# An expert layer's branches rearranged: the first up and its hint ahead of the arms, both products turned ahead of the third up, and the residual at an earlier place

## The chip, the cores and the metric

The kernel runs on one core of one Trainium2 chip. The metric is the device time of one execution in microseconds, the median of several runs. The kernel is a program of one core; its five engines are TensorE (PE in the profile), VectorE (DVE), ScalarE (ACT), GpSimd (POOL) and SyncE (SP), and each runs its own list of instructions in order. They wait for each other through semaphores.

## The reference

One decoder layer on 256 tokens of 1024 channels in float32: a token mixer, a cross-attention and a mixture of experts, each followed by a layer norm over the scaled residual. The change touches only the last part:

```python
def moe_ffn(x, router_w, router_b, w_gu, b_gu, w_dn, b_dn):
    logits = x2 @ router_w + router_b
    top_v, top_i = lax.top_k(logits, 4)          # 4 of 32 experts
    gate = jax.nn.softmax(top_v, axis=-1)
...
    def expert_block(args):
        gu = xb @ w_gu[e] + b_gu[e]              # 1024 -> 2048
        g, u = gu[:, :1024], gu[:, 1024:]
        g = jnp.minimum(g, 7.0); u = jnp.clip(u, -7.0, 7.0)
        h = (u + 1.0) * g * jax.nn.sigmoid(1.702 * g)
        return (h @ w_dn[e] + b_dn[e]) * gb[:, None]
...
x = layer_norm(alpha * x + moe_ffn(x), norm_g[2], norm_b[2])
```

Each expert has 8 MB of weights for the first product (gate and up, "gu") and 4 MB for the second ("down"), so the 32 experts read 384 MB. How many tokens an expert gets is known only when the router has run.

## The kernel before

The mixer and the attention take the first 370 us or so and are not touched. Behind them `Moe.run` goes through the 32 experts, in an order that begins at expert 16; "place e" below is the e-th expert in that order, from 0 to 31.

**Weights.** `load(e)` issues the 12 transfers of an expert, 1 MB each, on SP's queue: eight gu slots (line 1017), then four slots with a pair of down blocks each (line 1024). They go into a ring of 19 buffers of 1 MB, all called `w`. SP issues strictly in order, and a transfer into a buffer waits until the instructions that read the buffer's former content are over. With 12 slots for each place, slot n waits for the readers of slot n - 19: the eighth gu slot of place e + 1 waits for those of the first gu slot of place e. `ring_of(True)` takes a buffer out of the ring for good.

**The work of a place.** An expert's tokens are gathered in blocks. The first 32 are the "first up" (`upper(bank, 0, ..)`: 32 fp32 matmuls of line 1220 over the eight gu slots, which the trace records as 64, with a bias product of line 1224), then `act` (clipping, sigmoid and product on DVE and ACT, lines 1191 to 1199; its result is `uc`, the product), `hT_of` (transposes of line 91, which turn the product) and `rows_down` (16 matmuls of line 1265 over the down slots, 32 in the trace), with the sum into `ye` by ACT and DVE (line 1240). Every second place `combine` (line 1276) adds the outcome of the last two places into the output in four PSUM banks, and the other places gather the rows of the next two experts (`take`, line 1076, and `turn`, line 91, with the scaling of lines 1092 and 1094).

**The arms.** Since the count n of a place is data, each place has branches on PE, ACT and DVE: `If(n > 32)`, labelled `more`, with inside it `If(n > 64)`, labelled `most`. This gives three arms. None (n up to 32): first up, product, downs. Some (33 to 64): first up, second up of the next 32 tokens, two products, two downs. Many (over 64): as some, with a third block of 32 tokens that is gathered, turned, sent through the gu slots once more (the "third up", matmuls g<-w,xTo), and through the downs by `block_down`. In the trace a third up stands at three places only, 12, 16 and 25. In this kernel the first up stands inside each of the arms; a branch prefetch hint for the next place's branch, `soon(following)`, stands in each arm but the many arm, and one for `most` at the head of the `more` arm.

**The residual.** At place 20 (`MID`) `residual()` runs ahead of the loads: DVE spreads the norm's rows on diagonals (line 987), PE broadcasts them (line 990), ACT copies them to `gb`, and POOL makes the scaled residual `x2` (lines 994, 997). `gb` and `x2` are two buffers taken out of the ring for good, so it has 17 from there on. At places 22 and 24 `add` sums `x2` into the output banks (line 1009), at 22 POOL's queue brings the last norm's rows, and at 26 `last_rows` (line 1004) broadcasts them into `gb`. `finish` normalises the output after the last place; ahead of it stands a branch `rest` for counts over 96.

## Time and profile before

| | us |
|---|---|
| median of 3 runs | 1511.12 |
| lowest and highest run | 1500.52 to 1512.25 |
| the profiled execution's own time | 1505.24 |
| its span | 1503.3 |
| PE busy | 1240.6 (83%) |
| DVE busy | 612.3 (41%) |
| ACT busy | 360.4 (24%) |
| POOL busy | 137.6 (9%) |

The transfers moved 470.20 MB, on average 313 GB/s over the span. The span runs from the first instruction to the last one on the core. A row of a timeline gives the start, the duration, the engine, the line and operation, what is written and read (out<-in by the program's names, partitions x elements), the number of instructions in the row, and in brackets the idle time ahead of it with what ended it. "issue" there is time in which the engine waited for nothing that the profile shows. On SP's queue a row of transfers lasts from the first to the last issue of its group, the waits between them included.

### The profile page before, as it was taken

Reading aid. Unit: us, or ns where it says so; the run is one execution under the profiler, and the core shown is the slowest. Engines: PE = TensorE matmul, PEld = TensorE weight load, DVE = VectorE, ACT = ScalarE, POOL = GpSimd, SP = SyncE. Lnnn points to the kernel's source line nnn. Section 1 sums busy time; section 2 is a strip of 40 time slices with the busy share of each in tenths; the row PEclk is TensorE's granted clock in tenths of the full one; section 3 lists DMA queues with packets and bytes.
Section 4 is the critical chain, followed back from the end, with each engine's and each line's share of the span. In section 5 each row is a group of like instructions: output and inputs, shape, how many; then the busy total and the mean of one; then the engine's idle time right before and its main releaser. Section 6 shows DMA issues by size and latency. Waiting matters only on the chain. (4 is left out here: it accounts for less than half of the span.)

```text
span 1503.3 us, 21051 instructions
## 1 busy us (share of the span) xinstructions
PE 1240.6 (83%) x8396; PEld 614.9 (41%) x8396; DVE 612.3 (41%) x1346; ACT 360.4 (24%) x725; POOL 137.6 (9%) x139
## 2 busy tenths in 40 slices
PE   8878999999988877787779487859788888788774
PEld 8768979999852212221222132213222222222111
DVE  4999875685453222222222232214322323123124
ACT  4424564545331111111111011102211112112101
POOL 3993000000030000000000000000020000000001
PEclk9989999999978988989999799979899999699898
DMA  9526627656859999999996899779969998569991
GB/s 304 155 71 147 206 83 194 213 172 219 306 217 414 415 416 416 413 416 417 415 416 280 321 408 415 300 299 416 417 252 415 415 414 342 221 264 415 416 415 63
DMA packets 110187, 470.20 MB, mean 313 GB/s; under 512 B 12081, under 2 KB 16276, under 8 KB 77244
## 3 DMA queue, kind: packets, MB, share of 16 engines
q1 hardware_dynamic: 108028, 462.53, 78.7%
q0 software_dynamic: 1712, 4.26, 1.3%
q8 instruction: 114, 1.87, 0.5%
q10 hardware_dynamic: 272, 1.05, 0.2%
q14 instruction: 61, 0.50, 0.1%
HBM read 466.49 MB, written 1.31 MB: 311 GB/s over the span
## 5 line engine op out<-in xcount | busy, mean ns | idle before, releaser
L1220 PE MATMUL g<-w,xT 128*32 128x512 f32 x2048 | 291.3, 681 | 125.0 <-DMA w<-in_expert_w_gu_dram 62.6
L1265 PE MATMUL m<-w,hT 128*32 128x512 f32 x1472 | 213.4, 674 | 9.5 <-DVE ye L1240 6.2
L1220 PEld LDWEIGHTS g<-w,xT 128*32 128x32 f32 x2048 | 63.4, 118 | 326.8 <-issue 209.5
L1191 DVE TENSOR_SCALAR gc<-g 64x256 f32<-64x256 f32 x70 | 29.2, 416 | 378.4 <-PE g L1220 278.9
L142 DVE TENSOR_TENSOR wl<-w,wh 128x1024 fp32r<-128x1024 f32 (+1 forms) x96 | 114.4, 1228 | 67.8 <-ACT wh L80 67.8
L1192 ACT ACTIVATE row<-gc 64x256 f32<-64x256 f32 x92 | 38.4, 418 | 386.5 <-DVE gc L1191 386.5
L80 ACT ACTIVATE wh<-w 128x1024 fp32r<-128x1024 f32 (+1 forms) x112 | 105.8, 992 | 102.1 <-PE big L172 66.4
L1240 DVE TENSOR_TENSOR ye<-ye,m 32x512 f32<-32x512 f32 x86 | 58.5, 680 | 167.1 <-ACT ye L80 165.9
L172 PE MATMUL big<-xh,wh 128*128 128x256 f32 x352 | 102.3, 291 | 0.0
L172 PE MATMUL big<-xl,wh 128*128 128x256 f32 x352 | 101.8, 289 | 0.0
L172 PE MATMUL big<-xh,wl 128*128 128x256 f32 x352 | 101.8, 290 | 0.0
L1265 PEld LDWEIGHTS m<-w,hT 128*32 128x32 f32 x1472 | 48.4, 121 | 115.5 <-issue 97.4
L80 ACT ACTIVATE ye<-m 32x512 f32<-32x512 f32 x86 | 50.7, 590 | 176.1 <-PE m L1265 175.1
L1220 PE MATMUL u<-w,xT 128*32 128x512 f32 x704 | 82.1, 607 | 0.0
L91 PE MATMUL m<-ident,uc 64*128 64x64 f32 x172 | 29.0, 250 | 50.5 <-ACT hT L80 31.3
L172 PEld LDWEIGHTS big<-xl,wh 128*128 128x128 f32 x352 | 69.4, 197 | 1.1 <-issue 0.8
L172 PEld LDWEIGHTS big<-xh,wh 128*128 128x128 f32 x352 | 69.5, 198 | 0.3
L172 PEld LDWEIGHTS big<-xh,wl 128*128 128x128 f32 x352 | 69.0, 197 | 1.3 <-issue 1.2
L1276 PE MATMUL y<-ye,pgT 128*128 128x512 f32 x128 | 60.3, 613 | 3.1 <-DVE ye L1240 2.1
L994 POOL TENSOR_TENSOR w<-w,row 128x512 f32<-128x512 f32 x4 | 5.2, 1328 | 589.1 <-DMA w<-in_expert_w_gu_dram 589.1
L1092 DVE TENSOR_SCALAR xT<-m,rowc 128x128 f32<-128x128 f32 x64 | 22.1, 406 | 84.0 <-PE m L91 72.8
L91 PEld LDWEIGHTS m<-ident,uc 64*128 64x128 f32 x172 | 17.3, 140 | 86.1 <-ACT hT L80 44.2
(429 smaller groups left out, 1799.7 us busy)
## 6 DMA issues: line engine op xcount, KB each, us to landing
w<-in_expert_w_gu_dram SPq DMA_DIRECT2D x256, 1024.0 KB
w<-in_expert_w_down_dram SPq DMA_DIRECT2D x127, 1024.0 KB
w<-in_w_in_dram SPq DMA_DIRECT2D x23, 1024.0 KB
w<-in_xa_wkv_dram SPq DMA_DIRECT2D x8, 1024.0 KB
w<-in_w_branch_dram SPq DMA_DIRECT2D x4, 1024.0 KB
w<-in_w_out_dram SPq DMA_DIRECT2D x4, 1024.0 KB
w<-in_xa_wq_dram SPq DMA_DIRECT2D x4, 1024.0 KB
w<-in_xa_wo_dram SPq DMA_DIRECT2D x4, 1024.0 KB
```

Source lines behind the costliest of these rows:

```text
L80: self.nc.scalar.activation(out, in_, AF.Copy, scale=scale)
L91: self.nc.tensor.transpose(out, in_, self.ident[0:k, 0:k])
L142: eng.tensor_tensor(out=l[:, js, :n], in0=t[:, js, :n], in1=h[:, js, :n].bitcast(F32), op=ALU.subtract)
L172: self.last = nc.tensor.matmul(dst, l, r, start=(b not in seen), stop=(last and i == 2), skip_group_check=True)
L994: self.nc.gpsimd.tensor_tensor(out=x2[:, t, s], in0=self.x2h[:, t, s].bitcast(F32), in1=self.x2l[:, t, s].bitcast(F32), op=ALU.add)
L1092: self.nc.vector.tensor_scalar(out, in_, g, t, op0=ALU.mult, op1=ALU.add)
L1191: nc.vector.tensor_scalar_min(gc[0:n, s], g[:, s], 7.0)
L1192: nc.scalar.activation(sg[0:n, s], gc[0:n, s], AF.Sigmoid, scale=1.702)
L1220: nc.tensor.matmul(gu[32 * c:32 * c + 32, :], xT[:, k, :], W[k][:, c * 512:c * 512 + 512], start=(k == 0), stop=(k == 7), skip_group_check ...
L1240: nc.vector.tensor_add(ye[:, c, :], ye[:, c, :], pd[64 * c:64 * c + 32, :])
L1265: self.nc.tensor.matmul(pd[p0:p0 + w, :], hT[:, j, h * w:h * w + w], W[8 + k][:, c * 512:c * 512 + 512], start=(i < P // (2 * w)), stop=(i ...
L1276: self.nc.tensor.matmul(self.y[t][c][:], pgT[rows, t, :], ye[rows, v, :], start=False, stop=last, skip_group_check=True)
```

## The change

The diff does six things:

- `residual()` moves from ahead of the loads of place 20 to behind those of place 6, into two ring buffers that go back to the ring; both `add` follow at place 7, where before they were at 22 and 24.
- The two buffers that stay out of the ring, `gb` and `o`, are taken at place 31, behind its loads; the norm's rows come into a tile `ends` (the buffer of `xno`), and `last_rows` runs there, where before it was at 26.
- The first up of each place from 1 on stands ahead of the branch `more`, once, and no longer in both arms. Its hint, `soon(f"more{e}")`, stands just ahead of it. The hints at the ends of the arms, and the one for `rest`, are gone. Place 0 gets a hint `early`.
- In the many arm both products are turned (`hT_of`) into the halves of one tile `both` before the third up, and the gates of its rows (`gates_of`) are turned there too.
- In the many arm `act` of the third block stands ahead of the two downs, not between them.
- `rows_down` takes the turned product and no longer turns it itself.

```diff
...
 FIRST = 16
-MID = 20
+MID = 6
...
                 if when == k:
                     fn()
-    def rows_down(self, W, uc, r, between=()):
+    def rows_down(self, W, hT, r, between=()):
         nc = self.nc
-        hT = self.hT_of(uc, 32)
         pd = self.pm.tile([P, 512], F32, name="m")
         self.down(W, [(hT, 32, pd)], between)
         ye = self.ye[r:r + 32]
...
         for c in range(2):
             nc.vector.tensor_add(ye[:, c, :], ye[:, c, :], pd[64 * c:64 * c + 32, :])
-    def hT_of(self, uc, w):
+    def hT_of(self, uc, w, hT=None):
         nc, f = self.nc, self.f
         n = 2 * w
         b = self.pm.tile([P, 512], F32, name="m")
-        hT = self.wk.tile([P, 4, P], F32, name="hT")
+        if hT is None:
+            hT = self.tile("hT", [P, 4, P])
         for i in range(2):
             for j in (2 * i, 2 * i + 1):
                 f.transpose(b[:, j * n:j * n + n], uc[0:n, j * P:j * P + P])
...
         gu = self.up(e, W, blocks, self.places(blocks))[0]
         return self.act(gu, w, self.tile("uc", [P, 512], bufs=2))
-    def block_down(self, e, W, pe, uc, w, name="xno"):
-        pgT = self.gates_of(e, pe, w)
+    def block_down(self, e, W, pe, uc, w, name="xno", pgT=None):
+        if pgT is None:
+            pgT = self.gates_of(e, pe, w)
         pd = self.pm.tile([P, 512], F32, name="m")
         self.down(W, [(self.hT_of(uc, w), w, pd)])
         ye = self.tile(name, [P, D])
...
         nc.vector.tensor_copy(self.cnt[:, 0:E], self.cf[:])
         nc.vector.tensor_reduce(self.cnt[:, E:E + 1], self.cf[:], axis=AX.X, op=ALU.max)
         xT2 = xT, xT1
+        tc.mark_branch_hint_location("early", "LikelyTaken", engines=[ENG.PE])
         self.gather_T(pe, *xT2, 0)
         for t in range(2):
             for c in range(2):
...
             tc.mark_branch_hint_location(label, "LikelyTaken", engines=[ENG.PE])
+        def rows_of(keep=False):
+
+            return self.ring_of(keep)[:].rearrange("p a b -> p (a b)").rearrange("p (t d) -> p t d", t=2)
+
         count(0)
         for e in range(E):
-            if e == MID:
-                gb, x2 = (self.ring_of(True)[:].rearrange("p a b -> p (a b)").rearrange("p (t d) -> p t d", t=2) for _ in range(2))
-                self.residual(gb, x2)
             x = order[e]
             W = self.load(x, e == E - 1)
+            if e == MID:
+                gb, x2 = rows_of(), rows_of()
+                self.residual(gb, x2)
             first, end, lead = e == 0, e == E - 1, e % 2 == 0
             c = 0 if lead else CAP
             ahead = not lead and not end
...
                 for j, at in ((1, 0), (2, 2), (3, 4)):
                     hooks.append((at, lambda j=j: self.gather_T(pe0, *xT2, j)))
                 hooks.append((5, gates_all))
-            if e in (MID + 2, MID + 4):
-                self.add(x2, (e - MID) // 2 - 1)
-                if e == MID + 2:
-                    for i, name in enumerate(('norm_g', 'norm_b')):
-                        nc.gpsimd.dma_start(x2[i:i + 1, 0, :], self.I[name][2:3, :])
-            if e == MID + 6:
-                self.last_rows(gb, x2[0:2, 0, :])
+            if e == MID + 1:
+                for t in range(2):
+                    self.add(x2, t)
+            if end:
+                ends = self.tile("xno", [P, D])
+                for i, name in enumerate(('norm_g', 'norm_b')):
+                    nc.gpsimd.dma_start(ends[i:i + 1, :], self.I[name][2:3, :])
+                gb, o = rows_of(True), rows_of(True)
+                self.last_rows(gb, ends[0:2, :])
             if not end:
                 count(e + 1)
             bank, other = self.gu()
-            following = "rest" if end else f"more{e + 1}"
             product = lambda gu: self.act(gu, 32, self.tile("uc", [P, 512], bufs=2))
             def middle():
...
             if first:
-                with tc.If(n > 32):
+                with tc.If(n > 32, label="early"):
                     self.early(x, W, 32)
                     with tc.If(n > CAP):
                         self.early(x, W, CAP)
                 upper(bank, 0, hooks)
                 for t in range(2):
                     bias(t)
-                soon(following)
                 self.ye = self.tile("ye", [P, 2, 512])
                 nc.vector.memset(self.ye[:], 0.0)
                 uc = product(bank)
                 middle()
-                self.rows_down(W, uc, c, turns())
+                self.rows_down(W, self.hT_of(uc, 32), c, turns())
             else:
+                soon(f"more{e}")
+                upper(bank, 0, hooks)
                 with tc.If(n > 32, label=f"more{e}") as some:
                     soon(f"most{e}")
-                    upper(bank, 0, hooks)
                     peo = self.onehot(self.halves("peo", 32), [(x, CAP, 32, 0)])
                     uc = product(bank)
                     upper(other, 1)
                     uc2 = product(other)
                     with tc.If(n > CAP, label=f"most{e}") as many:
-                        xo, xTo = self.tile("xno", [P, D]), self.tile("xTo", [P, 8, 32])
+                        xo = self.tile("xno", [P, D])
                         for h in range(2):
                             self.take(peo, xo, h)
                         middle()
+                        both = self.tile("hT", [P, 4, P])
+                        hT = self.hT_of(uc, 32, both[:, :, 0:64])
+                        pgTo = self.gates_of(x, peo, 32)
+                        xTo = self.tile("xTo", [P, 8, 32])
                         for h in range(2):
                             self.turn(xo, xTo, h)
+                        hT2 = self.hT_of(uc2, 32, both[:, :, 64:128])
                         self.rows_up(W, xTo, bank, pk)
-                        self.rows_down(W, uc, c, turns())
                         rest = self.act(bank, 32, self.tile("xno", [P, D])[:, 0:512])
-                        self.rows_down(W, uc2, c + 32)
-                        self.block_down(x, W, peo, rest, 32)
+                        self.rows_down(W, hT, c, turns())
+                        self.rows_down(W, hT2, c + 32)
+                        self.block_down(x, W, peo, rest, 32, pgT=pgTo)
                     with many.Else():
-                        soon(following)
                         middle()
-                        self.rows_down(W, uc, c, turns())
-                        self.rows_down(W, uc2, c + 32)
+                        self.rows_down(W, self.hT_of(uc, 32), c, turns())
+                        self.rows_down(W, self.hT_of(uc2, 32), c + 32)
                 with some.Else():
-                    soon(following)
-                    upper(bank, 0, hooks)
                     uc = product(bank)
                     middle()
-                    self.rows_down(W, uc, c, turns())
+                    self.rows_down(W, self.hT_of(uc, 32), c, turns())
             if done and lead:
                 done = None
             if end:
...
```

How this moves instructions on PE is seen best in the order in which they stand. The first piece is the many arm of place 12 before the change, from the last `combine` matmul of the two places before on (y<-ye,pgT; uc is a product, xno in the row x8 the rows of the third block and in the row x4 its product, pg the gates):

```order
L1276 MATMUL y_4453<-ye,pgT 128x512
L91 MATMUL m<-ident,xno 128x32 x8
L1220 MATMUL g<-w,xTo 32x512 x20
L1224 MATMUL g<-bg,pk 64x512 x2
L1220 MATMUL g<-w,xTo 32x512 x12
L91 MATMUL m<-ident,uc 128x64 x4
L1265 MATMUL m<-w,hT 32x512 x16
L91 MATMUL m<-ident,uc 128x64 x4
L1265 MATMUL m<-w,hT 32x512 x16
L91 MATMUL m<-ident,pg 128x128 x2
L91 MATMUL m<-ident,xno 128x64 x4
L1265 MATMUL m<-w,hT 32x512 x16
```

Now, in the same arm:

```order
L1276 MATMUL y_4453<-ye,pgT 128x512
L91 MATMUL m<-ident,uc 128x64 x4
L91 MATMUL m<-ident,pg 128x128 x2
L91 MATMUL m<-ident,xno 128x32 x8
L91 MATMUL m<-ident,uc 128x64 x4
L1220 MATMUL g<-w,xTo 32x512 x20
L1224 MATMUL g<-bg,pk 64x512 x2
L1220 MATMUL g<-w,xTo 32x512 x12
L1265 MATMUL m<-w,hT 32x512 x32
L91 MATMUL m<-ident,xno 128x64 x4
L1265 MATMUL m<-w,hT 32x512 x16
```

The transposes of both products (uc) and of the gates (pg) stood behind the third up, each ahead of its down; now the first product and the gates come ahead of the transposes of the third block's rows, the second product behind them, and the third up is followed by both downs in a row.

The second piece is the passage from place 12 to the odd place 13, at the join behind the arms (the first row ends the none arm; cnt holds the counts), before:

```order
L1427 UNCONDITIONAL_BRANCH
L1351 TENSOR_LOAD cnt
L1351 ISA x2
L1427 COMPARE_AND_BRANCH
L1744 BRANCH_PREFETCH_HINT
L1220 MATMUL g<-w,xT 32x512 x20
L1224 MATMUL g<-bg,pk 64x512 x2
L1220 MATMUL g<-w,xT 32x512 x12
```

and now:

```order
L1435 UNCONDITIONAL_BRANCH
L1753 BRANCH_PREFETCH_HINT
L1353 TENSOR_LOAD cnt
L1353 ISA x2
L1220 MATMUL g<-w,xT 32x512 x20
L1224 MATMUL g<-bg,pk 64x512 x2
L1220 MATMUL g<-w,xT 32x512 x12
L1435 COMPARE_AND_BRANCH
L1753 BRANCH_PREFETCH_HINT
L1220 MATMUL u<-w,xT 32x512 x20
```

Before, the branch of place 13 was the next thing at the join, and the first up was found behind it, in each arm; now the hint and the first up stand at the join and the branch comes behind them.

The third piece is on PE at the head of the last place, where `last_rows` now stands (line 1004; line 1435 is the branch of place 30, then that of place 31):

```order
L1265 MATMUL m<-w,hT 32x512 x16
L1435 UNCONDITIONAL_BRANCH
L1753 BRANCH_PREFETCH_HINT
L1004 MATMUL m<-xno,ident 128x512 x4
L1220 MATMUL g<-w,xT 32x512 x20
L1224 MATMUL g<-bg,pk 64x512 x2
L1220 MATMUL g<-w,xT 32x512 x12
L1435 COMPARE_AND_BRANCH
L1753 BRANCH_PREFETCH_HINT
```

Before, a row of line 1004 stood ahead of the first up of place 26, and here only the branch. On POOL's queue the two transfers of the norm's rows stood between the branches of places 22 and 23; now they are behind those of place 30. The residual's four matmuls (line 990) stand in the same way at the join ahead of the first up of place 6, where before they stood ahead of the branch of place 20.

More of the change, by code (lines that the diff above doesn't have):

```diff
@@ L1471, in run @@
                 self.remainder(e, engines)
-        self.finish(gb, x2, out)
+        self.finish(gb, o, out)
     def early(self, e, W, base):
```

## The prediction

> **What bounds the kernel now.** I began with the table by stages, which shows busy time, granted clock, share of the transfers and GB/s in each stretch from place 1 on (columns: the stretch; its length and busy us of PE, PEld, DVE, ACT, POOL; clock; DMA share; GB/s).
>
> ```profile
> 460.00:797.00 337.00, 266.87 (x1690) 74.30 (x1692) 89.70 (x250) 49.79 (x112) 0.00 (x0) 0.89 1.02 415
> 797.00:880.00 83.00, 59.40 (x405) 18.67 (x398) 19.69 (x57) 12.30 (x30) 0.00 (x0) 0.88 0.78 309
> ...
> 940.00:1022.00 82.00, 58.38 (x374) 18.08 (x366) 18.04 (x53) 10.82 (x28) 0.00 (x0) 0.83 0.78 310
> ...
> 1080.00:1130.00 50.00, 42.38 (x249) 11.61 (x252) 15.42 (x42) 7.36 (x15) 11.90 (x6) 0.81 0.72 293
> ...
> 1250.00:1350.00 100.00, 78.57 (x492) 24.46 (x488) 25.42 (x73) 18.07 (x40) 0.00 (x0) 0.86 0.65 258
> 1350.00:1467.00 117.00, 87.97 (x538) 23.87 (x536) 28.34 (x78) 15.96 (x36) 0.00 (x0) 0.88 1.02 415
> ```
>
> The stream of weights runs at 415 GB/s nearly throughout, with a DMA share of 1.02: there the transfers are the bound, and no PE work is worth anything. A slot of 1.049 MB then takes 2.53 us, a place of 12 slots 30.3. Four stretches lie below it, and what they lose is length x (1 - rate/415): 83 x 0.255 = 21.2 us, 82 x 0.253 = 20.7, 50 x 0.294 = 14.7, 100 x 0.378 = 37.8; 94.4 in all. That is what a better order can win. Next came SP's queue, to see which issues are late there:
>
> ```profile
> 455.52 15.56 SPq L1017 DMA_DIRECT2D w<-in_expert_w_gu_dram  x8
> 476.13 16.78 SPq L1017 DMA_DIRECT2D w<-in_expert_w_gu_dram  x8
> ...
> 781.39 42.42 SPq L1017 DMA_DIRECT2D w<-in_expert_w_gu_dram  x8
> 833.64 29.34 SPq L1017 DMA_DIRECT2D w<-in_expert_w_gu_dram  x8
> ...
> 922.57 42.47 SPq L1017 DMA_DIRECT2D w<-in_expert_w_gu_dram  x8
> 975.36 30.48 SPq L1017 DMA_DIRECT2D w<-in_expert_w_gu_dram  x8
> ...
> 1065.46 42.57 SPq L1017 DMA_DIRECT2D w<-in_expert_w_gu_dram  x8
> ...
> 1280.25 48.51 SPq L1017 DMA_DIRECT2D w<-in_expert_w_gu_dram  x8
> ```
>
> Eight gu issues should take some 18 us; these take 29 to 48. The rows from 781.39 are the gu slots of places 13, 14, 17, 18, 21 and 27, each waiting for a buffer that a many arm (places 12, 16, 25) or the residual (20) holds. The last row waits for a combine: the sixth of its eight is the first that needs a buffer of place 26, with 17 left in the ring. Third, PE in the first of these arms and behind it:
>
> ```profile
> 812.41 4.50 PE L1220 MATMUL g<-w,xTo 128*32 128x512 f32 x40 [0.22 <-ACT xTo L1094]
> ...
> 820.57 0.33 PE L91 MATMUL m<-ident,uc 64*128 64x64 f32 x2
> ...
> 821.53 3.64 PE L1265 MATMUL m<-w,hT 128*32 128x512 f32 x32
> ...
> 830.00 0.34 PE L91 MATMUL m<-ident,uc 64*128 64x64 f32 x2 [4.57 <-ACT hT L80]
> 830.27 5.34 PE L1265 MATMUL m<-w,hT 128*32 128x512 f32 x32
> 839.17 0.30 PE L91 MATMUL m<-ident,pg 128*128 128x128 f32 x1 [3.56 <-DVE pg L1119]
> ...
> 846.93 1.99 PE L1276 MATMUL y<-xno,pgTo 64*128 64x512 f32 x8 [0.73 <-ACT xno L80]
> 860.67 6.52 PE L1220 MATMUL g<-w,xT 128*32 128x512 f32 x40 [11.75 <-issue]
> ...
> 868.13 2.78 PE L1220 MATMUL g<-w,xT 128*32 128x512 f32 x24
> ```
>
> PE stands still for 4.57 and 3.56 us for turned products and gates, ends the arm at 848.9, and then for 11.75 us waits for nothing that the profile shows: the arm has no hint, so PE jumps to the join, and there at once to another arm. Where work stood at the join ahead of a branch, at place 26, such a wait is much shorter (first row), and so it is after an arm with a hint (last row):
>
> ```profile
> 1300.37 7.16 PE L1004 MATMUL m<-w,ident 2*128 2x512 f32 x8 [4.21 <-issue]
> ...
> 1326.33 3.70 PE L1276 MATMUL y<-ye,pgT 128*128 128x512 f32 x8
> ...
> 1344.64 4.50 PE L1220 MATMUL g<-w,xT 128*32 128x512 f32 x40 [3.59 <-issue]
> ```
>
> **The arms, and place 12.** Ahead of the third up now stand one product's transposes, the gates' and, behind the rows' own, the other product's. Each product took two transposes of 0.33 with a copy of 0.4 between them, about 1 us; the gates' two and their wait take the rest of some 3. So the third up starts later, by 5.2 as I work it out (2 if the gates and copies hide behind each other, 7 if nothing does); it costs 8.2, from 812.41 to 820.57. Then both downs follow in a row (3.64 each) and hide the third block's `act`, which DVE does ahead of the first down's sum; only that block's transposes (1.0), its down (3.64 to 5.34) and the combine (0.73 + 1.99) are left. From 817.6 that is 8.2 + 7.3 + 1.0 + 5.3 + 2.7 = 24.5: the arm ends at 842.1, 6.8 earlier. The first up then stands at the join, one fetch away, and its branch's hint is 10 us ahead of the branch: I put 4.2 in place of 11.75 (bounds 0 and 11.75), 7.5 earlier.
>
> Against it stands how the buffers come back. Before, each gu matmul of a none arm's first up released its slot at once; since the releasing now belongs to what stands in the arms behind, all eight come together at PE's first instruction there, a take or a combine. The row of 833.64 ends at 862.98 with the slot that needs the first of place 13, 2.3 us after the first up began at 860.67; now it comes after the whole first up (10.2, from 860.67 to 870.9) and 0.4 of the take, 8.3 to 8.4 later. Sum: 6.8 + 7.5 - 8.4 = 5.9 us gained in this hole of 21.2.
>
> **Place 16** has the same arm. Its gap is 11.45, so 6.8 + 7.2 - 8.4 = 5.6, and PE was also behind the stream there:
>
> ```profile
> 930.25 3.71 PE L1220 MATMUL g<-w,xT 128*32 128x512 f32 x17 [3.03 <-issue]
> ...
> 1003.52 2.79 PE L1220 MATMUL g<-w,xT 128*32 128x512 f32 x12 [11.45 <-issue]
> ```
>
> The first row is the first up of place 16: ended by "issue", not by a transfer, so the weights lay there. Now PE leaves place 12 14.3 us earlier (6.8 + 7.5) and the stream only 5.9, so PE comes 8.4 nearer to it, and place 16 begins that much earlier against the stream (0 if PE had no lag to lose). I take 8.4: 14.0 of the hole of 20.7.
>
> **Place 25.** The ring now keeps 19 buffers, so the first slot that needs a buffer of place 26 is the eighth of place 27, not the sixth. Without the loss of 37.8 the sixth, which left with the first combine at about 1327.5, would have left at 1289.7, and the eighth at 1294.7. It will wait for place 26's first combine still: the arm, which ended at 1296.2, ends at 1289.4; + 4.2 + first up 10.2 + second up 8.3 + 0.6 = 1312.7. So 18.0 are lost and 19.8 gained (bounds: 12 with a gap of 11.6, 26 with none and a first up of 8.3).
>
> **The residual.** At place 20 it held PE from 1075.2 to 1087.9:
>
> ```profile
> 1070.22 5.00 PE L1265 MATMUL m<-w,hT 128*32 128x512 f32 x32 [0.78 <-DVE ye L1240]
> 1079.01 2.94 PE L990 MATMUL m<-xno,one 128*128 128x512 f32 x4 [3.79 <-DVE xno L987]
> ...
> 1087.86 5.57 PE L1220 MATMUL g<-w,xT 128*32 128x512 f32 x40
> ```
>
> Now place 20's slots come back with its first combine, at 1075.2 + 8.3 + 8.3 + 0.6 = 1092.4; the eighth of place 21, which left at 1108.0, would without the loss leave at 1108.0 - 14.7 = 1093.3. So the 14.7 go (12 if the first up is slow). At place 6 the same 12.6 us of DVE and PE in turns come back:
>
> ```profile
> 574.33 1.67 PE L1220 MATMUL g<-w,xT 128*32 128x512 f32 x8 [1.45 <-DMA w<-in_expert_w_gu_dram]
> ...
> 599.11 5.03 PE L1265 MATMUL m<-w,hT 128*32 128x512 f32 x32 [0.78 <-DVE ye L1240]
> 607.14 4.50 PE L1220 MATMUL g<-w,xT 128*32 128x512 f32 x40 [3.00 <-DMA w<-in_expert_w_down_dram]
> ```
>
> PE is done at 604.1 and waited 3.00 for weights: part of it is hidden. First up from 616.8 to 626.8, its slots back at 627.4. The sixth gu of place 7 needs the first (two buffers more are out for the residual); it is due 22 slots after the eighth of place 5, which PE read as it came: 574.3 + 22 x 2.53 = 630.0, so it must leave one to two transfers earlier, at 627.5 to 624.9. Loss 0 to 2.5; I take 2.5. POOL's part, which ended 10 us behind PE's, nobody waits for before place 7. Net 12.2.
>
> **What is lost.** Place 1 has neither take nor combine:
>
> ```profile
> 475.00 2.78 PE L1220 MATMUL g<-w,xT 128*32 128x512 f32 x24
> 480.16 0.30 PE L91 MATMUL m<-ident,uc 64*128 64x64 f32 x2 [2.38 <-DVE uc L1199]
> ```
>
> The eight slots from the last gu of place 2 on, which left from 471.1 (455.52 + 15.56) to about 480, come back only with the transposes at 480.5. The stream has by then used up what it had issued: 2 to 3 transfers after 471. I take a loss of 4.0 (0 to 9.4). At the end, `last_rows` stands ahead of the last first up:
>
> ```profile
> 1441.81 1.20 ACT L80 ACTIVATE ye<-m 32x512 f32<-32x512 f32 x2 [6.03 <-PE m L1265]
> ...
> 1461.71 4.47 PE L1220 MATMUL u<-w,xT 128*32 128x512 f32 x40
> ...
> 1490.01 1.30 DVE L1511 BATCH_NORM_STATS2 st<-y 128x6 f32<-128x512 f32 x2 [3.17 <-PEq L1469]
> w<-in_norm_g_dram POOLq DMA_DIRECT2D x1, 4.0 KB, 5.6
> ```
>
> POOL's transfers wait at the join for ACT's last copy, 1443.0; with 5.6 to landing and 0.4 to start, 1449; the four broadcasts took 7.16 at place 26, so 1456.2, and the first up, slow after the wait, ends at 1466.6 in place of 1461.7: 4.9 lost (0 if the rows come sooner, 8 if later). DVE waited for PE's branch ahead of the statistics; without its hint I add 1.0 (0 to 4.2). The `early` hint saves 0: its branch follows at once. The rearranged hints of the other places pay nothing, since the stream hides PE there.
>
> **Sum.** 5.9 + 14.0 + 19.8 + 12.2 - 4.0 - 4.9 - 1.0 = 42.0. The span goes from 1503.3 to 1461.3; the profiled execution, 1505.24, to 1463.2; the median, 5.9 above it, to 1469.1. I forecast 1467, between the two, since two of three runs lie 6 to 7 above the profiled one.
>
> **The rivals.** *No fetch at the join.* By the order of the instructions the many arm's end now jumps over 258 to 292 on PE, before over 403 to 430; if the target has already been fetched, 4.2 and the slow first up (1.9) go at three places: 18 less, 1449. Against it, the 3.59 of the quoted row came after a jump over fewer than 250. The Trainium skill ("Runtime: NRT & Kernel Launch", "Instruction fetch mechanics") has blocks of 256 instructions, two of them held, and a fetch for a taken branch beyond; a target 258 to 292 ahead could lie in the second block. By that rule 1449 could come; the 3.59 speaks against it.
>
> *The long gap stays.* If the 11.6 is one slow fetch, not two, three places lose 7.4 each: 22 more, 1489. For it: both measured gaps are near 11.6; against: the 4.21 after the same kind of arm.
>
> *Nothing to be seen.* The holes move: what place 12 and 16 win is lost again to slots held at other places until the stream, 384 MB at 415 GB/s, is as far behind as before. About 1503 to 1511; against it, at places with none PE waits for weights (the 3.00).
>
> *Slower.* The late lump. Should PE at a place be more than about 22 us behind the stream (30.3 less 2.5 to 5.1 for a transfer and 3 for the end of the first up), the slots given back after the first up come too late at every following place, at place 1's price of 4.0: 31 x 4.0 = 124, less the 46 gained elsewhere, 78 more: 1589. Against it, PE is free some 7 us a place.
>
> **Chances and range.** Forecast 0.56, with 1455 to 1480 of its own; no fetch 0.16; long gap 0.16; nothing 0.07; slower 0.05. The first three are all faster by over 1% (15 us, about what a measurement of this kernel tells from no change): 0.88, within 1% 0.07, slower 0.05. The range must hold the first three: 1441 (no fetch and the good ends at places 1 and 25) to 1496.
>
> **What would show it.** The stretches at places 20 and 21 full at 415; at places 12, 16 and 25 holes of about 15, 7 and 18 us; 4 us of idle PE ahead of the first up behind a many arm; two downs in a row with no wait there; SP's first wait after 471 ended by transposes; four broadcasts ahead of the last first up. I am wrong if SP waits in many other places, or if the gap stays near 11.6.

## The result and the profile after

| | before | changed |
|---|---|---|
| median, us | 1508.36 (4 runs, 1500.52 to 1512.25) | 1454.63 (4 runs, 1450.04 to 1461.55) |
| profiled execution, us | 1505.24 | 1461.55 |
| its span, us | 1503.3 | 1459.7 |

The ratio is 0.9654, with an interval from 0.959 to 0.9718: faster, as forecast. The median lies 12 below the forecast of 1467 and inside the range of 1441 to 1496. The profiled execution was the slowest of its four runs; it was expected at 1463.2 and took 1461.55. In a second series the same kernel took 1459.18 (5 runs, 1455.65 to 1461.01), ratio 0.9691 (0.9671 to 0.9711).

The stretches of the changed kernel, with the columns of the table of before:

```profile
460.00:600.00 140.00, 108.50 (x664) 28.50 (x656) 33.31 (x95) 17.15 (x39) 2.51 (x2) 0.86 0.98 398
600.00:660.00 60.00, 50.00 (x286) 15.34 (x278) 19.73 (x55) 10.94 (x24) 11.90 (x6) 0.89 0.88 354
...
797.00:900.00 103.00, 89.62 (x634) 28.85 (x630) 31.48 (x93) 17.77 (x41) 0.00 (x0) 0.93 0.87 352
...
960.00:1022.00 62.00, 50.81 (x370) 17.14 (x366) 17.67 (x47) 10.43 (x23) 0.00 (x0) 0.97 0.95 386
1022.00:1240.00 218.00, 182.88 (x1240) 52.98 (x1236) 65.28 (x186) 36.49 (x83) 0.00 (x0) 0.91 1.01 414
1240.00:1330.00 90.00, 80.31 (x588) 25.60 (x584) 29.93 (x80) 16.90 (x38) 0.00 (x0) 1.00 0.87 348
```

The same reckoning as before, length x (1 - rate/415), gives the holes that are left: 5.7 us behind place 1, 8.8 at places 6 and 7, 15.6 behind place 12, 4.3 behind 16, 14.5 behind 25, and nothing at places 20 and 21, which lie in the fifth row. (A hole is time in which the stream of weights falls below its full rate.) Before there were 94.4 us of holes; now there are 48.9. SP's queue shows the same from the other side (eight gu slots in a row, of places 2, 7, 13, 14, 18, 21 and 27):

```profile
451.63 26.09 SPq L1017 DMA_DIRECT2D w<-in_expert_w_gu_dram  x8
...
599.34 36.07 SPq L1017 DMA_DIRECT2D w<-in_expert_w_gu_dram  x8
...
790.86 36.32 SPq L1017 DMA_DIRECT2D w<-in_expert_w_gu_dram  x8
834.15 33.95 SPq L1017 DMA_DIRECT2D w<-in_expert_w_gu_dram  x8
...
967.86 25.21 SPq L1017 DMA_DIRECT2D w<-in_expert_w_gu_dram  x8
...
1053.70 21.41 SPq L1017 DMA_DIRECT2D w<-in_expert_w_gu_dram  x8
...
1245.41 37.66 SPq L1017 DMA_DIRECT2D w<-in_expert_w_gu_dram  x8
```

The row of place 21 has fallen from 42.57 to 21.41, that of place 2 has grown from 15.56 to 26.09, and place 7 has a new long one. PE in the many arm of place 12 and behind all three:

```profile
821.06 0.33 PE L91 MATMUL m<-ident,pg 128*128 128x128 f32 x1 [1.04 <-DVE pg L1119]
...
824.86 7.22 PE L1220 MATMUL g<-w,xTo 128*32 128x512 f32 x40
...
835.62 7.05 PE L1265 MATMUL m<-w,hT 128*32 128x512 f32 x64
...
845.45 3.64 PE L1265 MATMUL m<-w,hT 128*32 128x512 f32 x32 [0.79 <-DVE ye L1239]
849.80 1.99 PE L1276 MATMUL y<-xno,pgTo 64*128 64x512 f32 x8 [0.72 <-ACT xno L80]
857.14 6.44 PE L1220 MATMUL g<-w,xT 128*32 128x512 f32 x40 [5.36 <-DMA w<-in_expert_w_gu_dram]
...
981.59 4.50 PE L1220 MATMUL g<-w,xT 128*32 128x512 f32 x40
...
1264.92 4.50 PE L1220 MATMUL g<-w,xT 128*32 128x512 f32 x40
```

The waits of 4.57 and 3.56 are gone (1.04 is left ahead of the gates) and both downs run as one row. From the end of the second up (813.65) to the last combine (851.79) the arm takes 38.1 us, before 42.8; the arms of places 16 and 25 take 38.0 and 41.3, before 45.9 and 46.2. The wait ahead of the next first up is 5.36 at place 12, put down to a transfer that had been issued some 30 us or more before (SP's row of 790.86 ends at 827.18), and none at all at places 16 and 25.

Places 5 and 6, where the residual now stands, the start of place 0 (behind its branch, line 1420) and the last place:

```profile
589.09 0.77 PE L1076 MATMUL m<-w,pe 128*128 128x512 f32 x1 [3.63 <-DVE uc L1199]
...
614.39 2.80 PE L990 MATMUL m<-xno,one 128*128 128x512 f32 x4 [3.79 <-DVE xno L987]
...
623.10 5.71 PE L1220 MATMUL g<-w,xT 128*32 128x512 f32 x40
...
632.97 3.70 PE L1276 MATMUL y<-ye,pgT 128*128 128x512 f32 x8
```

```profile
437.82 1.93 PE L1220 MATMUL g<-w,xT 128*32 128x512 f32 x8 [1.07 <-PEq L1420]
```

```profile
1400.93 7.16 PE L1004 MATMUL m<-xno,ident 2*128 2x512 f32 x8 [7.95 <-DMA xno<-in_norm_b_dram]
...
1417.34 3.19 PE L1220 MATMUL u<-w,xT 128*32 128x512 f32 x28
```

PE is 6.3 us later at place 6's first up than I had it (616.8), though the work is as forecast; 3.63 of that is a new wait at the head of place 5's arm, and the takes and the down behind it ran at a granted clock of 0.58 (589 to 600). At place 31 PE waits 7.95 for the norm's rows; from the second up to the end it takes 42.4, before 41.6.

### The profile page after: what moved, and what is told of

Same layout as the page of the kernel before. It is cut to its first block, busy times and chain, and to the rows that moved or that the text cites. A ratio compares the mean times of both kernels' runs of the same rounds, so it can differ in the third digit from the quotient of the medians.

```text
span 1459.7 us, 21030 instructions
## 1 busy us (share of the span) xinstructions
PE 1231.6 (84%) x8396; PEld 609.8 (42%) x8396; DVE 608.7 (42%) x1346; ACT 359.8 (25%) x725; POOL 137.2 (9%) x139
## 5 line engine op out<-in xcount | busy, mean ns | idle before, releaser
L1220 PE MATMUL g<-w,xT 128*32 128x512 f32 x2048 | 283.3, 665 | 82.2 <-DMA w<-in_expert_w_gu_dram 81.1
L1265 PE MATMUL m<-w,hT 128*32 128x512 f32 x1472 | 204.3, 640 | 16.5 <-DVE ye L1239 8.6
L1220 PEld LDWEIGHTS g<-w,xT 128*32 128x32 f32 x2048 | 59.7, 115 | 278.0 <-DMA w<-in_expert_w_gu_dram 140.4
L1276 PE MATMUL y<-ye,pgT 128*128 128x512 f32 x128 | 63.4, 641 | 8.2 <-issue 6.2
L320 DVE SCALAR_TENSOR_TENSOR cy<-cu,cp,cy 128x256 f32<-128x256 f32 x90 | 47.8, 584 | 0.1
```

Source lines behind the costliest of these rows:

```text
L320: eng.scalar_tensor_tensor(y[:, m, :], u[:, m, k:k + S], scale, y[:, m, :], op0=ALU.mult, op1=ALU.add)
L1220: nc.tensor.matmul(gu[32 * c:32 * c + 32, :], xT[:, k, :], W[k][:, c * 512:c * 512 + 512], start=(k == 0), stop=(k == 7), skip_group_check ...
L1265: self.nc.tensor.matmul(pd[p0:p0 + w, :], hT[:, j, h * w:h * w + w], W[8 + k][:, c * 512:c * 512 + 512], start=(i < P // (2 * w)), stop=(i ...
L1276: self.nc.tensor.matmul(self.y[t][c][:], pgT[rows, t, :], ye[rows, v, :], start=False, stop=last, skip_group_check=True)
```

## The experiments

The two halves of the change were taken back first, each alone.

**The old many arm.**

```diff
-both = self.tile("hT", [P, 4, P])
-hT = self.hT_of(uc, 32, both[:, :, 0:64])
-pgTo = self.gates_of(x, peo, 32)
...
-hT2 = self.hT_of(uc2, 32, both[:, :, 64:128])
 self.rows_up(W, xTo, bank, pk)
+self.rows_down(W, self.hT_of(uc, 32), c, turns())
 rest = self.act(bank, 32, self.tile("xno", [P, D])[:, 0:512])
-self.rows_down(W, hT, c, turns())
-self.rows_down(W, hT2, c + 32)
-self.block_down(x, W, peo, rest, 32, pgT=pgTo)
+self.rows_down(W, self.hT_of(uc2, 32), c + 32)
+self.block_down(x, W, peo, rest, 32)
```

> The many arm has its old order again (each product and the gates turned behind the third up, ahead of its own down; the third block's act between the two downs); all else is as in the changed kernel. Theory: the new order shortens the arm, from the end of the second up to the last combine, by some 5 us (42.8 before, 38.1 now, places 12, 16 and 25), and what bounds the stream at these three places is the end of the arm: about 5 us lost at each, 15 in all, 1470 in place of 1455. Rival: the arm's length is not what counts, only the first up at the join; then the time stays at 1455.

Measured 1474.13 (1473.75 to 1479.54), ratio 0.9795 (0.976 to 0.9831). The interval lies above both of the changed kernel's. SP's rows of places 14, 18 and 27:

```profile
827.93 47.39 SPq L1017 DMA_DIRECT2D w<-in_expert_w_gu_dram  x8
...
967.38 39.08 SPq L1017 DMA_DIRECT2D w<-in_expert_w_gu_dram  x8
...
1249.93 50.66 SPq L1017 DMA_DIRECT2D w<-in_expert_w_gu_dram  x8
```

The changed kernel has 33.95, 25.21 and 37.66 there; a part of the 13 in each is made good by shorter rows ahead of them. From the end of the second up to the last combine the three arms take 44.2, 44.8 and 46.6 us, in the changed kernel 38.1, 38.0 and 41.3: together some 18 more, and the span is 18.0 longer, 1477.7. The theory holds, the rival falls: the arm's end does set the time.

**The first up in the arms again.**

```diff
-soon(f"more{e}")
-upper(bank, 0, hooks)
 with tc.If(n > 32, label=f"more{e}") as some:
     soon(f"most{e}")
+    upper(bank, 0, hooks)
...
 with many.Else():
+    soon(following)
...
 with some.Else():
+    soon(following)
+    upper(bank, 0, hooks)
```

> The first up of each place stands in both arms again, with the hints for the next branch at the arms' ends as before; the many arm, the residual and the last rows are as in the changed kernel. Theory: the idle time ahead of the first up behind a many arm comes back, 11 us for 5.4 at place 12 and 11 for 0 at place 16, 4 for 0 at place 25, but slots are given back one by one during the first up, 8.4 earlier: by these the stream gains 3 at place 12, loses 3 at 16 and 4 to 8 at 25, and wins back the 6 of place 1. The sum is near nothing: 1450 to 1460. Rival: moving the first up ahead is where the gain lies; then 20 or more are lost, 1475 and over.

Measured 1468.48 (1461.57 to 1471.27), ratio 0.9743 (0.9698 to 0.9788): between the two. PE ahead of the first up behind places 12, 16 and 25:

```profile
851.71 3.75 PE L1220 MATMUL g<-w,xT 128*32 128x512 f32 x20 [9.32 <-issue]
...
986.18 7.55 PE L1220 MATMUL g<-w,xT 128*32 128x512 f32 x40 [11.99 <-DMA w<-in_expert_w_gu_dram]
...
1274.13 6.31 PE L1220 MATMUL g<-w,xT 128*32 128x512 f32 x40 [5.29 <-issue]
```

The waits came back as expected (9.32 for 5.36, 11.99 for 0, 5.29 for 0), and place 2's row of eight issues fell from 26.09 to 18.93. What I had wrong is the sum. The row of place 26 took 46.31 for 29.24: the arm of place 25 was no longer than in the changed kernel (41.2, 41.3), but PE came to it later against the stream, since place 24's first up stood for 3.04 and 2.95 in its arm. And the hole of places 6 and 7 went too, though the residual stands at place 6 in this kernel as well; the row of place 7, 36.07 in the changed kernel:

```profile
594.25 19.21 SPq L1017 DMA_DIRECT2D w<-in_expert_w_gu_dram  x8
```

By the starts of SP's rows, set against the changed kernel's, some 6 us are gained at place 1 and 8 at places 6 and 7, and 2, 5 and 14 are lost behind places 12, 16 and 25. So in the profiles the first up ahead of the arms is worth some 10 net (span 1469.4 for 1459.7), and it pays at places 16 and 25; in time the intervals of the two kernels overlap.

**Where the residual stands.** `MID = 20` and `MID = 8` for `MID = 6`.

> MID is 20 again: the residual behind the loads of place 20, in two ring slots that go back, both add at 21; all else as changed. Theory: the hole at places 6 and 7 (8.5 us of the stream by the changed kernel's trace) goes, and the old hole of some 15 at places 20 and 21 returns, so 6 lost: 1461. Rival: with slots that go back and the ring's 19 buffers the hole at 20 was one of the ring's size; then it stays away and the time falls to about 1447.

Measured 1456.23 (1449.79 to 1458.42), ratio 0.9668 (0.9624 to 0.9712). Its stretches around places 6 and 20:

```profile
580.00:660.00 80.00, 62.22 (x398) 19.44 (x390) 22.23 (x61) 13.89 (x31) 0.00 (x0) 0.91 1.02 416
...
1040.00:1110.00 70.00, 60.48 (x358) 18.20 (x350) 21.93 (x61) 10.73 (x22) 11.93 (x6) 0.86 0.92 370
```

No hole at place 6; at place 20 one of 70 x (1 - 370/415) = 7.6 us, half of what it was. Theory and rival were each half right: about half of the old 14.7 does not come back with the residual. That this half was the ring of 17 is likely but not shown alone, since the first up and the place of the loads differ too. The place of the residual moves a hole of about 8 and the sum stays.

> MID is 8: the residual stands behind two places with the none arm (6 and 7), where PE comes to the join ahead of the stream, and no longer behind place 5, whose some arm ends late. Theory: its 12.6 us on PE are then covered but for a few, and the hole of 8.5 us of places 6 and 7 shrinks to 0 to 3: 6 to 8 gained, 1448. Rival: the hole comes from the two slots that the residual holds until the add, wherever it stands; then 8 are lost at places 8 and 9 and the time stays at 1455.

Measured 1455.33 (1454.69 to 1458.39), ratio 0.9678 (0.9641 to 0.9714); its stretches around places 6 and 8:

```profile
580.00:660.00 80.00, 60.84 (x377) 19.13 (x370) 25.14 (x66) 14.11 (x32) 2.69 (x2) 0.89 1.02 416
660.00:800.00 140.00, 120.17 (x776) 34.73 (x778) 41.81 (x116) 22.61 (x50) 11.90 (x6) 0.90 1.02 415
```

In the trace the theory holds: the residual's POOL work stands in the second row and costs the stream nothing, and the span is 1452.9 where the two profiles of the changed kernel have 1459.7 and 1459.2. The timed median is not below the changed kernel's first series; against its second the interval overlaps. That the edit is worth its 7 in time is not shown by this run alone.

**The last rows earlier.**

```diff
-            if end:
+            if e == 28:
                 ends = self.tile("xno", [P, D])
```

> The norm's rows, last_rows and the two slots that stay out of the ring are taken at place 28 and no longer at 31; all else as changed. Theory: at place 31 PE waits 7.95 us for POOL's transfer and 7.16 for the four broadcasts, and the stretch from the last slot's landing to the end grew by 6.0 us; at place 28 PE waits for weights anyway, so 6 are gained: 1449. Rival: the ring of 17 that is left from place 28 on costs a hole of its own, as large or larger: 1455 or over.

Measured 1451.1 (1448.65 to 1458.57), ratio 0.965 (0.9598 to 0.9701). At place 28 PE, then SP's row of place 29:

```profile
1323.51 7.16 PE L1004 MATMUL m<-xno,ident 2*128 2x512 f32 x8 [7.12 <-DMA xno<-in_norm_b_dram]
```

```profile
1312.40 31.98 SPq L1017 DMA_DIRECT2D w<-in_expert_w_gu_dram  x8
```

The wait stays with the four broadcasts, 14.3 us together, more than PE had to spare: place 29's row takes 31.98, in the changed kernel 18.04. Place 31's row then begins 3.2 later (1377.41 for 1374.26), but from there to the end it takes 6.2 less, so the span falls by 3.0 in all. Both were partly right, and in time the gain isn't clear of the intervals.

**No hint at place 0.**

```diff
-        tc.mark_branch_hint_location("early", "LikelyTaken", engines=[ENG.PE])
-                with tc.If(n > 32, label="early"):
+                with tc.If(n > 32):
```

> The hint for the branch of place 0 is taken out; all else as changed. Theory: this hint, which I had put at nothing, is why place 0's first up began earlier (1.07 us behind PE's queue in place of 2.95) and place 1's gu slots landed 4.5 us earlier than before: 2 to 4.5 lost, 1457 to 1459, with the wait of about 3 us ahead of the first up of place 0 in the trace. Rival: these 4.5 are the scatter of the mixer and attention ahead of it; then the wait comes back but place 1's slots land as in the changed kernel, within 1 us of the wait's length or less, 1455.

Measured 1456.78 (1454.0 to 1462.47), ratio 0.9693 (0.9636 to 0.9749). Its first up at place 0:

```profile
440.82 1.94 PE L1220 MATMUL g<-w,xT 128*32 128x512 f32 x8 [4.09 <-PEq L1419]
```

The wait came back, 4.09 for 1.07, and the first up began 3.0 later. The time is the changed kernel's within its scatter, so the hint does shorten the wait and the run ends no sooner: SP's row of place 2 begins 1.5 later than in the changed kernel (453.17 for 451.63), but that of place 3 only 0.2 (480.85 for 480.69), so what place 0 gains is waited for again behind place 1. My theory of this run falls, and the nothing of the prediction stands.

**Place 1 in the arms.**

```diff
+inside = e == 1
+if not inside:
     soon(f"more{e}")
     upper(bank, 0, hooks)
```

(with the first up in both arms where `inside` holds, and `soon("more1")` at place 0)

> At place 1 alone the first up stands in both arms again, with the hint at place 0; all else as changed. Theory: the slots of places 2 and 3 that the lump at the transposes of place 1 gave back late come one by one again, and the loss of 5.6 us of the stream between places 1 and 2 goes: 1449. Rival: the stream at place 2 is late for another reason, the slow start of place 0, and nothing is gained: 1455.

Measured 1451.67 (1449.42 to 1455.72), ratio 0.9654 (0.96 to 0.9708). SP's row of place 2:

```profile
451.06 19.22 SPq L1017 DMA_DIRECT2D w<-in_expert_w_gu_dram  x8
```

19.22 for 26.09: the price of the lump at place 1 (eight buffers given back at once), some 6 us, is shown. The theory holds in the trace; in time the gain isn't clear of the intervals, since a wait of 5.40 behind place 25, which the changed kernel doesn't have, took some of it back.

**Where the code lies.** That wait, and the 5.36 behind place 12 with none behind 16 and 25, asked for an experiment that moves code and changes no work.

```diff
 with tc.If(n > CAP):
     self.early(x, W, CAP)
+    b = self.pm.tile([P, 512], F32, name="m")
+    for _ in range(65):
+        f.transpose(b[:, 0:P], f.ident[:])
```

> 65 transposes (130 PE instructions) are added to the arm of place 0 for counts over 64, which never runs here; they shift all of PE's later code by 130 instructions and change nothing that is executed. Theory: whether PE finds the join behind a many arm in its held code depends on where the arm's end lies in the blocks of 256 that the transfers of instructions show (16.4 KB each): counted from the first instruction, the end of the arm of place 12 lies at 0.78 of a block and stalled 5.4 us, those of 16 and 25 at 0.27 and 0.08 and did not. Shifted by 130 of 256 the ends lie at 0.29, 0.78 and 0.59: the stall of 5 us goes at place 12 and comes up at 16. The time stays within 3 of 1455. Rival: place 12 has it for another reason (its neighbours, its counts); then it keeps its 5.4 and 16 stays at 0.

Measured 1468.18 (1461.86 to 1472.71), ratio 0.9759 (0.9698 to 0.982). Behind place 16 and behind 25:

```profile
976.67 6.93 PE L1220 MATMUL g<-w,xT 128*32 128x512 f32 x40 [5.03 <-issue]
```

```profile
1258.92 1.05 PE L1220 MATMUL g<-w,xT 128*32 128x512 f32 x3
1262.79 4.49 PE L1220 MATMUL g<-w,xT 128*32 128x512 f32 x37 [2.82 <-issue]
```

The wait went from place 12, whose first up now begins with no idle time, to place 16, as the theory said. Behind place 25 PE runs three records and then stands for 2.82: as I read it, it found the join in its held code but not what comes next. I was wrong on the time, by 13 us (the interval overlaps those of the changed kernel a little): I had looked at three places, and the jumps to the arms have their blocks too. PE's waits put down to issue, summed over the run (us, times, longest), in this kernel:

```profile
PE y L1276 <- issue: 14.0, 4, 5.0
PE g L1220 <- issue: 7.8, 2, 5.0
...
PE m L1076 <- issue: 5.3, 1, 5.3
```

In the changed kernel these were 6.2 us in 2 waits of line 1276; the 5.36 stands there under another name. Not every such wait costs time. SP's row of place 31, and PE at place 30:

```profile
1370.98 19.00 SPq L1017 DMA_DIRECT2D w<-in_expert_w_gu_dram  x8
```

```profile
1385.70 6.42 PE L1276 MATMUL y<-ye,pgT 128*128 128x512 f32 x8 [4.32 <-issue]
```

In spite of its waits the stream is 3.3 us ahead of the changed kernel's here (1370.98 for 1374.26), and the span is 4.9 longer: from there to the end it takes 93.6 for 85.4. So in this profile the loss lies at the end, where the combine of place 30 waited 4.32 and took 6.42 for 3.70, ahead of the last rows.

From both kernels I counted which targets lie in the last eighth of a block of 256 instructions, and shifted by 84 (`range(42)`).

> The changed kernel with 42 transposes (84 PE instructions) in the arm of place 0 that never runs; nothing that is executed changes. In the traces so far PE stood 1 to 5 us behind a jump when the target lay in the last eighth of a block of 256, up to about 0.775 counted from the first instruction, or when the jump came just over that border. By this the changed kernel has such targets at places 10, 12, 18 and 20, the one shifted by 130 at 9, 14, 16, 22, 25, 30 and 31. Theory: shifted by 84 only places 3, 23 and 28 have one, where PE waits for weights anyway: no gap over 1 us behind the many arms and fewer such waits in all; 3 to 6 faster than the changed kernel in the same call, some 1450. Rival: a shift by itself costs time, as 130 did, by something else than blocks: 1460 or more.

> The changed kernel once more, as a measure for the other two on the same chip, and with a second profile. Theory: 1455 within 4, a hole of 6 to 9 us of the stream at places 6 and 7, a wait ahead of place 13's first up between 0 and 5.4 us, and none behind places 16 and 25. Rival: the hole at places 6 and 7 belonged to the one profiled execution; then it is below 3.

Both ran on one chip: 1453.41 (1452.27 to 1458.25, ratio 0.9667, 0.9646 to 0.9689) against the changed kernel's 1459.18, so 5.8 us less by the medians, with intervals that overlap a little. In the shifted kernel the first up behind place 12 no longer waits, and nor does place 5's arm; behind places 16 and 25 PE stands for 1.40 and 1.11 in the midst of the first up, a little more than expected. Waits were moved rather than removed: places 3 and 4 now have 4.43 and 4.21, where SP's rows stay at 18 to 19 us. Places 5 and 6:

```profile
585.19 0.50 PE L1076 MATMUL m<-w,pe 128*128 128x512 f32 x1
...
616.82 5.65 PE L1220 MATMUL g<-w,xT 128*32 128x512 f32 x40
```

With that the residual ends where the prediction had it (616.8), and place 7's row takes 31.31 for 36.07. In the changed kernel's second profile place 5's arm waited 3.77, so 3.63 was no accident, and place 7's row took 36.54. Its other waits were there again too: 4.97 behind place 12, none behind 16 and 25, 1.80 and 4.15 at places 10 and 18. The kernel with the last rows at place 28 has the same code on PE as far as place 28 and waited 1.56 behind place 12, so the length differs between executions with the same code (near a block's border, as I read it). Without the hint at place 0, which is one instruction less, it was 0.94.

**Together.** `MID = 8`, place 1 in its arms, 82 transposes, and at the end:

```diff
-            if end:
-                ends = self.tile("xno", [P, D])
+            if e == 28:
+                gb, o = rows_of(True), rows_of(True)
                 for i, name in enumerate(('norm_g', 'norm_b')):
-                    nc.gpsimd.dma_start(ends[i:i + 1, :], self.I[name][2:3, :])
-                gb, o = rows_of(True), rows_of(True)
-                self.last_rows(gb, ends[0:2, :])
+                    nc.gpsimd.dma_start(o[i:i + 1, 0, :], self.I[name][2:3, :])
+            if e == 29:
+                self.last_rows(gb, o[0:2, 0, :])
```

> Four edits at once: the residual at place 8, place 1's first up in its arms again, the norm's rows brought at place 28 into a buffer that stays out of the ring and broadcast at 29 (at 28 both stood in a row and PE waited), and 82 transposes in the arm that never runs, so that no target ahead of a first up behind a many arm lies at a block's end. Theory: 7 for the residual, 5 for place 1, 5 for the last rows, 3 for the shift: 20 below the changed kernel, 1435. Rival: the gains at places 1 and 8 only bring the stream nearer to the holes of places 12, 16 and 25, which then take them back, since there the end of the arm sets the time: 1445 to 1452.

Measured 1444.47 (1438.25 to 1445.55), ratio 0.9598 (0.9579 to 0.9617), with the changed kernel at 0.9691 (0.9671 to 0.9711) on the same chip: 14.7 us less, clear of both intervals. SP's rows of places 2, 7, 14 and 29:

```profile
451.71 18.54 SPq L1017 DMA_DIRECT2D w<-in_expert_w_gu_dram  x8
...
593.71 19.01 SPq L1017 DMA_DIRECT2D w<-in_expert_w_gu_dram  x8
...
817.59 29.16 SPq L1017 DMA_DIRECT2D w<-in_expert_w_gu_dram  x8
...
1293.14 22.48 SPq L1017 DMA_DIRECT2D w<-in_expert_w_gu_dram  x8
```

The holes at places 2 and 7 are gone and that at 29 is small. The profiled execution, the fastest of its five, gained what the theory said (span 1436.4 for 1459.2, 22.8 less; but the latter was the slowest of its five); the median gained 5 less than the 20 of the theory. By the starts of SP's rows in these two profiles each edit brought about its share: 5.4 at place 1, 7.0 with the residual, 5.7 behind place 12, and 4.5 behind the start of place 31. The rows behind places 12, 16 and 25 are about as long as in the changed kernel (place 14 29.16, 18 27.05, 27 38.63), so in this profile nothing was taken back there and the rival's reason does not hold. Which of the four edits brings less than its share in the other executions is open.

The two halves that were taken back alone are 18 and 10 of the 43.6 us of span. What the ring of 19 buffers in place of 17 is worth at place 25, which the prediction counted on, no run takes back alone.

## Why the prediction was right, step by step

- **Place 12**: 5.9 forecast, 21.2 - 15.6 = 5.6 measured, though two of its parts came out worse, by 3.3 together. The arm got 4.7 shorter, not 6.8: the third up took 10.8 (824.86 to 835.62), since it began with matmuls at the slow rate (7.22 for 40 records, before 4.50), where I had priced it from the row of before; the granted clock from 824 to 833 was 0.64. And the wait was 5.36, not 4.2. The price of the lump came out as forecast: SP's last gu slot of place 14 left 10.96 behind the start of the first up (868.10, 857.14), before 2.31, so 8.65 later. What made up for the 3.3 is in part the reckoning, which is no finer than a slot of 2.53: by the starts of SP's rows of places 13 and 16 (781.39 and 892.00 before, 790.86 and 897.10 now) the gain is 4.4. The rest stays open.
- **Places 16 and 25**: 14.0 and 19.8 forecast, 20.7 - 4.3 = 16.4 and 37.8 - 14.5 = 23.3 measured. The mechanisms were right, the term of the fetch was too large: 0 and 0 in place of 4.2 each. The arms got 7.9 and 4.9 shorter, where 6.8 was forecast for each. The rival without a fetch held at these two places. The rule of the Trainium skill that was weighed there ("Runtime: NRT & Kernel Launch", "Instruction fetch mechanics": blocks of 256 instructions, a fetch when a taken branch leaves the held ones) fits this: the runs with 130 and 84 more instructions moved the wait from 12 to 16 and took it away. What I held against it, the 3.59 after a shorter jump, was no counter-proof if, as these runs suggest, it depends on where the target lies in its block and not only on the length of the jump.
- **The residual**: 12.2 forecast, 14.7 - 8.8 = 5.9 measured. This is the step that failed. The 14.7 went as forecast; "Loss 0 to 2.5" at place 6 became 8.8. A part of that is place 5's arm, which the prediction took from the profile of before: it began 3.63 late and ran on at a granted clock of 0.58, where the run shifted by 84 has no wait and 1.00. With that shift place 7's row was some 5 shorter. The rest is not the wait: in the stretch from 580 to 660 three runs without it still have holes of 3.9, 4.4 and 6.0 (shift by 84, place 1 in its arms, shift by 130), by the same reckoning that gives the changed kernel 8.7, and the run without the hint at place 0 has 5.8 with a wait of 3.48. Of the kernels with the residual at place 6 only the one with the first ups in the arms has none, so the rest goes with the lump behind place 6's first up; the prediction had this lump in its sum and put its loss at 2.5 at most.
- **Place 1**: 4.0 lost forecast, 5.7 measured; the run with place 1 in its arms gave it back in its trace.
- **The end**: 4.9 + 1.0 lost forecast. The broadcasts began 6.65 behind ACT's last copy (1400.93, 1394.28), where 6.0 was forecast, and from the second up to the end it took 42.4 for 41.6. How long the wait would be if only its transfers were earlier was not tried alone.
- **The hint at place 0**: nothing forecast. It saved 3.0 there and nothing that the time shows at the end.

Place 2's row began 3.9 earlier than before (451.63, 455.52); no term of the forecast stands for that, and 1.5 of it at most is the hint's (453.17 without it). With it these make 3.9 + 5.6 + 16.4 + 23.3 + 5.9 - 5.7 = 49.4; the span fell by 43.6, and the 5.8 between are left for the end, where 4.9 + 1.0 was forecast. So the profiled execution came within 2 us of its forecast, by errors of 2 to 6 in single terms with both signs that cancel: the sum is in part luck. The rest of the 12 by which the median lies below the forecast is scatter: the forecast put the median 3.8 above the profiled execution, and it came 6.9 below it, since that execution was the slowest of its series. Of the rivals, the long gap did not happen, and nor did a late lump at every place: beside the holes that were priced with it, only place 1 paid the lump.

## What to carry to other kernels

Where a stream of transfers bounds a kernel, measure each hole by length x (1 - rate/full rate), find which release ends it, and price every edit by what it does to that release, the time in which it would have been needed included. Work moved out of branches can change when its buffers are counted as free, from one by one to all at once: behind place 12 this took 8.65 of the gain, and it was a loss at place 1 (5.7) and at the residual, where PE had no slack. In code with data-dependent branches, look at where jump targets lie before crediting or blaming an edit with 5 us: 130 instructions that never ran cost 9 to 13 us by the medians here and 84 gained some 4 to 6, both with intervals that overlap the changed kernel's a little, and one wait went from one place to another in the traces.

## What the runs showed of the hardware

- Behind some taken jumps on PE the first instruction came 5.0 to 5.4 us later (5.36 and 4.97 in the changed kernel, 5.03 with the shift by 130, 5.40 with place 1 in its arms). At one join PE ran three records and then stood 2.82.
- With the same code up to that place the wait behind place 12 was 5.36, 4.97 and 1.56 in three executions.
- Such a wait can be put down to a semaphore that the instruction had no need to wait for: the 5.36 carries the name of a transfer issued some 30 us or more before, and the 3.63 that of `uc`, which was done at 588.83, 0.26 ahead of the take; in the run shifted by 84 the same take began at 585.19, with `uc` done at 590.02. That these are waits for code is inferred from their going away with a shift that changes no work.
- Behind the wait of 3.63 the granted clock was 0.58 for the next 11 us; in the run without the wait it was 1.00 there.
